# Pool mixer by band matrices on TensorE, and two chunks of the output projection as native four-byte products

## The chip, the cores and the metric

The kernel runs on one NeuronCore of a Trainium2 chip, batch 1. The metric is the device time of one execution in microseconds. Engines are named as in the profile: PE is TensorE, DVE VectorE, ACT ScalarE, POOL GpSimd, SP the engine whose queue issues every load.

## The reference

A sequence of 256 tokens of width 1024 goes through two transformer blocks. The first has stick-breaking and latent attention, a gated feed-forward part with a short convolution, and a per-token embedding gate. The second block, in which the change lies, computes

```
z   = (rmsnorm(x) * (1 + sc1) + sh1) @ w_in
y_conv = silu(layernorm(depthwise_conv31(val * sigmoid(gate))))   # 256 channels
y_att  = sparse attention: top 64 keys of each query by an index score   # 512 channels
y_pool = pool mixer of u_pool                                     # 256 channels
x  = x + g1 * (concat(y_conv, y_att, y_pool) @ w_out)
x  = x + g2 * mixture_of_experts(rmsnorm(x) ...)   # 32 experts, two of them for a token
out = rmsnorm(x)
```

The pool mixer has four groups of 64 channels with windows w = 2, 4, 8, 16. For each it computes the mean over the last min(t + 1, w) tokens minus the token itself, multiplies the 64 channels by a 64 x 64 matrix and scales them:

```
y_pool[t, group] = ((cs[t] - cs[t - w]) / min(t + 1, w) - u[t]) @ pool_w[group] * pool_scale
```

## The kernel before

Tokens come in two blocks of 128 (TB[b]), channels in chunks of 128. Weights arrive as 1 MB loads into three raw buffers (pool wr). For most products a weight is split into two halves that TensorE takes in one pass (hi, a cast by ScalarE, and lo, the rest, a subtraction by VectorE; function split, recorded on line 291), and so are the activations; mm3 (lines 273 to 275) then makes three products, hi x hi, hi x lo and lo x hi. Some products take four-byte operands as they are ("native"); the profile shows each of these as two records.

The order of TensorE's work is written out by hand: ORDER is a list of steps. Those that the text speaks of are `ix` (index scores), `cv` (conv inputs), `up` (the pool branch's input projection), `qk`, `va` (queries, keys and values), `d` (attention scores), `sm` (softmax), `po` (pool weights), `w0` to `w3` (load and split of the output weights, two chunks a load), `dT` (transposes of the attention weights), `do` (attention output), `c60` (chunk 6 of the output projection, block 0; chunks 0 and 1 are the conv's, 2 to 5 the attention's, 6 and 7 the pool's), `tp` (conv taps), `ct` and `co` (conv norm and output), and `ea`, `eh`, `el`, `e1` to `e4`, `es` (load a piece of the experts' weights into a buffer that has become free). Engines other than TensorE and the loads are put in order by a scheduler before the kernel runs, by priority (the order of the program) and by its own estimate of times; then each engine works strictly in that order. A buffer or a bank is given to the next user when the last reader of the one before is done. There are eight banks of PSUM: four take one block's scores, four the output projection's sums.

Index scores give 64 keys of each query: VectorE finds eight maxima and takes them out, eight times over (lines 1268 and 1269), for each block. Their mask goes into the maxima of the attention scores (line 803), whose exponentials, sums and normalised weights are ScalarE's, but for the negated maximum (line 806) and the reciprocal (line 810).

The Pool branch: `up_proj` makes the 256 channels with tokens along the free axis; GpSimd sums windows by shifted additions and a division (lines 1331 to 1341), `pool_out` multiplies by pool_w (line 1349) and splits the result into chunks 6 and 7 of mix2. The conv's 31 taps are multiply-adds of VectorE (line 1298); of the second half of its channels the last N_TAP taps are products of ScalarE (`pr`, six buffers) that GpSimd adds up (`cb`, line 1308).

The mixture of experts reads 192 pieces of 1 MB (`ew`), each into the next buffer of a ring. The ring is made of buffers of the mixer as they become free: its 23 pieces stand in ORDER and after it, in the order in which they are issued.

Of the kernel before, what the change touches and what calls it, by code (L numbers as in the profile page):

```python
# [38 lines left out]
N_TAP = 12  # L39
# [10 lines left out]
ORDER = 'qi0 kT0 qi1 kT1 ix0 ix1 cv0 li0 li1 cv1 ea ea lo0 lo1 ae lw ea ea ea va0 up eh el qk0 qk1 qk2 qk3 va1 d0 sm0 d1 po sm1 w3 e1 e2 c60 c61 w1 dT0 do0 c70 c71 c20 w2 dT1 c30 do1 tp e3 e4 e4 rl g1 c21 c31 c40 w0 ct e1 e1 c50 c51 c41 es es co'  # L50
# [17 lines left out]
def block_pair_kernel(ctx, tc, A, out, dbg=None):  # L68
# [126 lines left out]
    winv = cp.tile([P, 2], F32, name="winv")  # L195
    for i, wdt in enumerate((2, 4, 8, 16)):
        G.memset(winv[64 * (i % 2):64 * (i % 2) + 64, i // 2:i // 2 + 1], 1.0 / wdt)
    rcp = cp.tile([P, 2, PW], F32, name="rcp")
    G.iota(rcp[:, 0, :], pattern=[[1, PW]], base=1, channel_multiplier=0, allow_small_or_imprecise_dtypes=True)
    V.reciprocal(rcp[:, 0, :], rcp[:, 0, :])  # L200
    V.tensor_scalar(rcp[:, 1, :], rcp[:, 0, :], winv[:, 1:2], None, op0=ALU.max)
    V.tensor_scalar(rcp[:, 0, :], rcp[:, 0, :], winv[:, 0:1], None, op0=ALU.max)
# [1109 lines left out]
    TS = slice(PW, PW + SEQ)  # L1312
    pw = wk.tile([P, 2, 64], F32, name="pw")
    load(pw, A["pool_w"])
    pooled = []

    def up_proj():
        upb = bank("pup")
        raw = raw_pk("w_in2_c", 4, (2, KC, P), "r_up")
        for j in range(2):  # L1320
            ch_unit(raw[:, j], upb[:, j * SEQ:(j + 1) * SEQ], hZ, f"w_up2{j}")
        pu, s_a, s_b = [w2k2(nm).rearrange("p (c t) -> p c t", c=2) for nm in ("pu", "s_a", "s_b")]
        for t_ in (pu, s_a, s_b):
            G.memset(t_[:, :, 0:PW], 0.0)
        S.copy(pu[:, :, PW:], upb.rearrange("p (c t) -> p c t", c=2))

        def sh(t, c, rs, k):
            return t[rs, c, PW - k:PW + SEQ - k]

        full, top = slice(0, P), slice(64, P)  # L1330
        G.tensor_tensor(s_a[:, :, TS], pu[:, :, TS], pu[:, :, PW - 1:PW + SEQ - 1], op=ALU.add)
        G.tensor_tensor(s_b[:, 1, TS], sh(s_a, 1, full, 0), sh(s_a, 1, full, 2), op=ALU.add)
# [588 lines left out]
```

## Time and profile before

| | us |
|---|---|
| median of 3 runs | 942.63 (941.95 to 943.38) |
| the profiled execution | 942.79 |
| its span | 941.1 |
| PE busy | 785.0 |
| DVE busy | 466.7 |
| ACT busy | 321.8 |
| POOL busy | 110.1 |

The busy times are sums over the whole span. The mixer of the second block lies between about 380 and 490 us, the experts behind it. Times in the rows are microseconds from the start of the span.

### The profile page before, as it was taken

To read this page: it belongs to the slowest core of one execution; us is meant where nothing else is said; L and a number is where in the kernel's file an instruction comes from. 1 tells how busy PE (TensorE), PEld (TensorE's weight loads), DVE (VectorE), ACT (ScalarE), POOL (GpSimd) and SP (SyncE) were. 2 spreads that over 40 slices of the span, in tenths; PEclk is the share of its full clock that TensorE was granted. 3 is DMA by queue.
4 is the path that set the end of the run, shared out by engine and by line. 5 is a ranking of instruction groups with operands and counts; after the bars stand their busy time and mean duration, and the time that the engine had idled before them with its cause. 6 is when DMAs were issued, how large, how long until landed. Compare 5 with 4: busy or idle time off the path is not lost. (4 is left out here: it accounts for less than half of the span.)

```text
span 941.1 us, 17238 instructions
## 1 busy us (share of the span) xinstructions
PE 785.0 (83%) x7172; PEld 570.9 (61%) x7172; DVE 466.7 (50%) x1011; ACT 321.8 (34%) x636; POOL 110.1 (12%) x176
## 2 busy tenths in 40 slices
PE   6999989999999998996988988677766767766864
PEld 6898859999999775894675645243333433433422
DVE  5777476678888788589963323112121121211113
ACT  5649645555555575465741101000010000100100
POOL 1321320222112112207010000000000000000000
PEclk9999999999999998997999999879799897988887
DMA  8862388588676755745389999999999999999994
GB/s 309 283 206 85 122 333 318 194 338 313 254 276 231 268 203 194 301 168 179 129 332 422 422 420 425 419 425 421 423 422 422 425 422 422 423 421 426 420 423 166
DMA packets 45894, 301.22 MB, mean 320 GB/s; under 512 B 5360, under 2 KB 6388, under 8 KB 11124
## 3 DMA queue, kind: packets, MB, share of 16 engines
q1 hardware_dynamic: 45812, 300.08, 79.9%
q8 instruction: 58, 0.95, 0.4%
q14 instruction: 24, 0.20, 0.1%
HBM read 299.01 MB, written 1.05 MB: 319 GB/s over the span
## 5 line engine op out<-in xcount | busy, mean ns | idle before, releaser
L1710 PE MATMUL eu<-ew,XT 128*32 128x256 f32 x2048 | 141.8, 409 | 51.6 <-DMA ew<-in_exp_dram 51.5
L1710 PEld LDWEIGHTS eu<-ew,XT 128*32 128x32 f32 x2048 | 60.9, 115 | 123.9 <-DMA ew<-in_exp_dram 57.0
L80 ACT ACTIVATE hm<-eu 128x128 f32<-128x128 f32 x32 | 8.9, 278 | 334.2 <-PE eu L1710 334.2
L1737 PE MATMUL ey<-ew,hmT 128*32 128x256 f32 (+2 forms) x1088 | 80.7, 432 | 37.1 <-DMA ew<-in_exp_dram 25.2
L1723 DVE TENSOR_TENSOR hm<-hm,eu 128x128 f32<-128x128 f32 x32 | 9.2, 288 | 145.4 <-ACT hm L80 145.4
L1737 PEld LDWEIGHTS ey<-ew,hmT 128*32 128x32 f32 x1088 | 33.1, 121 | 71.6 <-DMA ew<-in_exp_dram 34.8
L1748 DVE TENSOR_TENSOR eys<-ey,g2y 128x256 f32<-128x256 f32 x31 | 13.2, 425 | 107.5 <-PE ey L1737 107.5
L1008 POOL TENSOR_TENSOR ac<-cv_g,cv_v 128x256 f32<-128x256 f32 x22 | 36.0, 1637 | 154.3 <-ACT w_g_w L80 108.3
L222 POOL TENSOR_SCALAR ep_fin<-msf 128x2 f32<-128x2 f32 x1 | 0.2, 238 | 446.2 <-DVE msf L1827 446.2
L275 PE MATMUL u<-hF_h,w_g_w 128*128 128x256 f32 x168 | 47.6, 283 | 0.0
L273 PE MATMUL u<-hF_h,w_g_w 128*128 128x256 f32 x168 | 47.5, 283 | 0.0
L274 PE MATMUL u<-hF_l,w_g_w 128*128 128x256 f32 x168 | 47.5, 283 | 0.0
L274 PE MATMUL u<-hF_l,w_v_w 128*128 128x256 f32 x160 | 45.3, 283 | 0.0
L275 PE MATMUL u<-hF_h,w_v_w 128*128 128x256 f32 x160 | 45.3, 283 | 0.0
L273 PE MATMUL u<-hF_h,w_v_w 128*128 128x256 f32 x160 | 45.2, 283 | 0.0
L1639 PE MATMUL moe<-eys,gT 32*128 32x256 f32 (+1 forms) x528 | 43.4, 444 | 1.4 <-DVE eys L1761 1.4
L1720 DVE COPY gT<-pgs 128x256 f32<-128x256 f32 x32 | 13.6, 425 | 52.4 <-PE pgs L1706 52.3
L80 ACT ACTIVATE XT<-px,c_SH,c_G 128x128 f32<-128x128 f32 x32 | 14.7, 458 | 63.9 <-DVE XT L1681 63.9
L1673 PEld LDWEIGHTS px<-hr,x 128*128 128x128 f32 x256 | 33.0, 212 | 4.3 <-issue 3.3
L1673 PE MATMUL px<-hr,x 128*128 128x128 f32 x256 | 34.7, 299 | 0.7 <-DVE hr L1665 0.7
L274 PE MATMUL dn<-w_dn_w,ach 128*128 128x512 f32 x88 | 34.6, 393 | 0.0
L1639 PEld LDWEIGHTS moe<-eys,gT 32*128 32x128 f32 x528 | 28.8, 216 | 9.5 <-issue 7.0
(566 smaller groups left out, 1978.1 us busy)
## 6 DMA issues: line engine op xcount, KB each, us to landing
ew<-in_exp_dram SPq DMA_DIRECT2D x189, 1024.0 KB, 19.7
r_mod<-in_mod_w_dram SPq DMA_DIRECT2D x24, 1024.0 KB, 8.7
r_gv<-in_w_up_dram SPq DMA_DIRECT2D x22, 1024.0 KB, 6.3
r_d<-in_w_down_dram SPq DMA_DIRECT2D x11, 1024.0 KB, 5.0
r_wo<-in_w_o_dram SPq DMA_DIRECT2D x4, 1024.0 KB, 4.8
r_pg<-in_w_ple_gate_dram SPq DMA_DIRECT2D x4, 1024.0 KB, 6.1
r_out<-in_w_out_dram SPq DMA_DIRECT2D x4, 1024.0 KB, 4.8
r_v<-in_w_in_t_dram SPq DMA_DIRECT2D x2, 1024.0 KB, 7.2
```

The source lines that it names most:

```text
L80: i = getattr(nc.scalar, name)(*a, **kw)
L273: T.matmul(o, l[0], r[0], start=start, stop=False, skip_group_check=True)
L274: T.matmul(o, l[0], r[1], start=False, stop=False, skip_group_check=True)
L275: T.matmul(o, l[1], r[0], start=False, stop=stop, skip_group_check=True)
L1008: G.tensor_tensor(a_, gt, vl, op=ALU.mult)
L1639: T.matmul(moe[c][:, b * 256:b * 256 + 256][:, js], gT[rs, TB[b]], yt[rs, js], start=(start and b == 0), stop=stop, skip_group_check=True)
L1673: T.matmul(pt[:, j * P:(j + 1) * P], x[b][:, k * P:(k + 1) * P], hr[:, b], start=(b == 0), stop=(b == 1))
L1710: T.matmul(u[32 * g_:32 * g_ + 32, 0:2 * P], XT[:, k, 32 * i:32 * i + 32], etiles[6 * e + k // 2][k % 2][:, :, P * g_:P * g_ + P], start=( ...
L1720: V.tensor_copy(gT, pg[:, :SEQ])
L1723: V.tensor_mul(hm, hm, u[:, P:2 * P])
L1737: T.matmul(y[32 * c:32 * c + 32, 0:64 * (js.stop - js.start)], hmT[:, 32 * k:32 * k + 32], w2e[k].rearrange("p j (c i) -> p c j i", c=4)[: ...
L1748: V.tensor_mul(yt, y[:, 0:256], g2y)
```

## The change

The window means become products with band matrices. A matrix `band` of each window has 1/w on its w diagonals, less one on the main one; `edge` holds the first 16 columns of the first block, where fewer than w tokens exist. They are built once by GpSimd and VectorE. `up_proj` now gives tokens along the partitions (puT), `pool_band` multiplies them by the bands, with the result again in channels by tokens, and `pool_out` leaves one four-byte tile (mixP) in place of two halves. Chunks 6 and 7 of the output projection multiply mixP by the rows of w_out as they were loaded; those rows are not split, and their raw buffer is read until the last such product. N_TAP goes from 12 to 20. In ORDER a step `pb` (pool_band) stands behind `qk1`, and `po` before `d1` in place of after it. Casts of the other output weights are ordered behind the last score copies (`first=[list(qk_ins)]`, an order on ScalarE alone).

```diff
-N_TAP = 12
+N_TAP = 20
...
-ORDER = '... up eh el qk0 qk1 qk2 qk3 va1 d0 sm0 d1 po sm1 w3 e1 e2 c60 c61 w1 dT0 do0 c70 c71 c20 w2 dT1 ...'
+ORDER = '... up eh el qk0 qk1 pb qk2 qk3 va1 d0 sm0 po d1 sm1 w3 e1 e2 c60 c61 w1 dT0 do0 c70 c71 c20 w2 dT1 ...'
...
-    winv = cp.tile([P, 2], F32, name="winv")
...
-    V.tensor_scalar(rcp[:, 0, :], rcp[:, 0, :], winv[:, 0:1], None, op0=ALU.max)
...
+    WIN = (2, 4, 8, 16)
+    band, edge = wk.tile([P, 4, P + 16], F32, name="band"), wk.tile([P, 4, 16], F32, name="edge")
+    rt = wk.tile([P, 16], F32, name="rt")
+    G.iota(rt, pattern=[[1, 16]], base=1, channel_multiplier=0, allow_small_or_imprecise_dtypes=True)
+    V.reciprocal(rt, rt)
+    for i, wdt in enumerate(WIN):
+        G.memset(band[:, i], 1.0 / wdt)
+        V.tensor_scalar(edge[:, i], rt, 1.0 / wdt, None, op0=ALU.max)
+    for t_, n in ((band, P + 16), (edge, 16)):
+        G.affine_select(t_, t_, pattern=[[0, 4], [1, n]], compare_op=ALU.is_ge, fill=0.0, base=0, channel_multiplier=-1)
+        for i, wdt in enumerate(WIN):
+            if wdt < n:
+                G.affine_select(t_[:, i], t_[:, i], pattern=[[-1, n]], compare_op=ALU.is_ge, fill=0.0, base=wdt - 1,
+                                channel_multiplier=1)
+        m = min(n, P)
+        V.tensor_sub(t_[:, :, :m], t_[:, :, :m], ident[:, None, :m].to_broadcast([P, 4, m]))
+    puT, pooled, mixP = [w2k2(nm)[:, :2 * SEQ].rearrange("p (c t) -> p c t", c=2) for nm in ("puT", "pooled", "mixP")]
...
     def up_proj():
-        upb = bank("pup")
-        raw = raw_pk("w_in2_c", 4, (2, KC, P), "r_up")
-        for j in range(2):
-            ch_unit(raw[:, j], upb[:, j * SEQ:(j + 1) * SEQ], hZ, f"w_up2{j}")
...
+        raw = raw_pk("w_in2_u", 0, (KC, 256), "r_up")
+        o = [bank(f"pup{b}") for b in range(NB)]
+        tok_unit(raw, 256, [t[:, :256] for t in o], hZ, "w_up2")
+        for b in range(NB):
+            S.copy(puT[:, b], o[b][:, :256])
+
+    def pool_band():
+        pb = bank("pband")
         for c in range(2):
...
+            o = pb[:, c * SEQ:(c + 1) * SEQ]
+            for b, cs_, t_, j in ((0, slice(0, 16), edge, 0), (0, slice(16, P + 16), band, 16), (1, slice(P, SEQ), band, 0)):
+                for par in range(2):
+                    rs = slice(64 * par, 64 * par + 64)
+                    T.matmul(o[rs, cs_], puT[:, b, 128 * c + 64 * par:][:, :64],
+                             t_[:, 2 * c + par, j:j + cs_.stop - cs_.start], start=(c == b == 0 and t_ is edge),
+                             stop=True, skip_group_check=True)
+        S.copy(pooled, pb.rearrange("p (c t) -> p c t", c=2))
...
-                hi, lo = [t[rs, 6 + c, :] for t in mix2]
-                act(hi, src, AF.Copy, scale=g_)
-                V.scalar_tensor_tensor(lo, src, g_, hi.bitcast(F32), op0=ALU.mult, op1=ALU.subtract)
+                act(mixP[rs, c, :], src, AF.Copy, scale=g_)
...
+        qk_ins[:] = [S.copy(q2[0][:, c, :], o[:, :SEQ]), S.copy(k2T[:, c, :], o[:, SEQ:])]
...
     def out_weights(u):
         raw = raw_rows("w_out_2", u, f"r_out{u}")
+        if u == 3:
+
+            wpo.update({6 + j: raw[:, j, :] for j in range(2)})
+            return
         for j in range(2):
-            wpo[2 * u + j] = split(raw[:, j, :], f"w_out{2 * u + j}", (D,), eng=G if 2 * u + j in OUT_G else V)
+            wpo[2 * u + j] = split(raw[:, j, :], f"w_out{2 * u + j}", (D,), eng=G if 2 * u + j in OUT_G else V,
+                                   first=[list(qk_ins)])
...
-        row_unit(wpo[c], [t[:, c, TB[b]] for t in mix2], acc[b], b not in begun, False)
+        if c < 6:
+            row_unit(wpo[c], [t[:, c, TB[b]] for t in mix2], acc[b], b not in begun, False)
+        else:
+            for n in range(2):
+                T.matmul(acc[b][n], mixP[:, c - 6, TB[b]], wpo[c][:, H2[n]], start=b not in begun, stop=False,
+                         skip_group_check=True)
```

## Rows read from the trace of the kernel before

**Rows 1.** The page's slices: GB/s moved in each fortieth of the span.
```profile
GB/s 309 283 206 85 122 333 318 194 338 313 254 276 231 268 203 194 301 168 179 129 332 422 422 420 425 419 425 421 423 422 422 425 422 422 423 421 426 420 423 166
```

**Rows 2.** Windows: stretch, length, busy of PE, PEld, DVE, ACT, POOL; clock, DMA share, GB/s.
```profile
425.00:435.00 10.00, 6.82 (x38) 4.95 (x38) 10.00 (x26) 6.41 (x15) 9.53 (x10) 0.90 0.61 210
...
445.00:450.00 5.00, 4.14 (x9) 2.84 (x10) 4.89 (x20) 4.04 (x12) 0.00 (x0) 0.50 0.00 2
450.00:465.00 15.00, 14.04 (x101) 10.41 (x99) 13.79 (x32) 12.44 (x31) 0.73 (x1) 0.99 0.14 45
465.00:480.00 15.00, 15.00 (x83) 11.88 (x81) 9.36 (x22) 7.27 (x12) 1.59 (x4) 1.00 1.00 391
480.00:485.00 5.00, 5.00 (x29) 4.15 (x27) 4.63 (x8) 2.55 (x7) 1.03 (x2) 1.00 0.40 165
```

**Rows 3.** SP's queue: two issues (timeline), a wait (total, times, longest), r_out's landing time.
```profile
461.76 0.33 SPq L142 DMA_DIRECT2D ew<-in_exp_dram  x1
...
484.34 0.33 SPq L142 DMA_DIRECT2D ew<-in_exp_dram  x1
...
SPq L142 <- PE ppt_d L827: 22.7, 1, 22.7
...
r_out<-in_w_out_dram SPq DMA_DIRECT2D x4, 1024.0 KB, 4.8
```

**Rows 4.** Timeline of PE: start, us, engine, line, operation, count, idle before and its releaser.
```profile
442.71 1.54 PE L1349 MATMUL ppl<-s_a,pw 64*64 64x256 f32 x6 [4.14 <-POOL s_a L1341]
...
448.11 0.63 PE L274 MATMUL mo<-w_out_w,mix_h 128*128 128x512 f32 x1
448.54 0.63 PE L275 MATMUL mo<-w_out_w,mix_l 128*128 128x512 f32 x1
...
450.92 0.27 PE L827 MATMUL ppt_d<-ident,es 128*128 128x128 f32 x1
```

**Rows 5.** The page's slices: POOL's busy tenths.
```profile
POOL 1321320222112112207010000000000000000000
```

**Rows 6.** Timeline of ACT.
```profile
430.67 1.04 ACT L80 CAST w_out_w<-r_out 128x1024 fp32r<-128x1024 f32 x1 [2.40 <-DMA r_out<-in_w_out_dram]
...
441.28 0.40 ACT L80 ACTIVATE es<-es,nm_d 128x128 f32<-128x128 f32 x1 [6.49 <-DVE nm_d L806]
...
445.85 2.45 ACT L80 ACTIVATE es<-es,rc_d 128x128 f32<-128x128 f32 x8 [0.18 <-DVE rc_d L810]
```

**Rows 7.** Timeline of DVE.
```profile
417.87 1.22 DVE L291 TENSOR_TENSOR w_out_w<-r_out,w_out_w 128x1024 fp32r<-128x1024 f32 x1
...
424.32 1.41 DVE L291 TENSOR_TENSOR w_out_w<-r_out,w_out_w 128x1024 fp32r<-128x1024 f32 x1
...
438.41 0.27 DVE L803 CUSTOM_DVE_ANT_0 es<-sc_d,ixb 128x128 f32<-128x128 f32 x1
...
441.06 4.65 DVE L1298 SCALAR_TENSOR_TENSOR ca<-upad,cols,ca 128x256 f32<-128x256 f32 x9
...
445.63 0.19 DVE L810 RECIPROCAL rc_d<-sum_d 128x8 f32<-128x8 f32 x1
```

**Rows 8.** Timeline of PE: native products, and three-pass products at full clock.
```profile
427.34 1.03 PE L1370 MATMUL pq<-lv,r_wu 128*128 128x256 f32 x4
428.20 0.59 PE L1371 MATMUL pq<-lv,r_wu 128*128 128x256 f32 x2
428.63 1.02 PE L1377 MATMUL pv<-r_wu,lv 128*128 128x512 f32 x2
...
454.41 0.40 PE L275 MATMUL mo<-w_out_w,mix_l 128*128 128x512 f32 x1
454.64 0.39 PE L273 MATMUL mo<-w_out_w,mix_h 128*128 128x512 f32 x1
```

**Rows 9.** Groups of POOL: count, busy us, mean ns, idle before them by releaser.
```profile
L1308 POOL TENSOR_TENSOR cb<-cb,pr 128x256 f32<-128x256 f32 x11 | 9.5, 866 | 3.1 <-ACT pr L80 2.3
...
L1008 POOL TENSOR_TENSOR ac<-cv_g,cv_v 128x256 f32<-128x256 f32 x22 | 36.0, 1637 | 154.3 <-ACT w_g_w L80 108.3 <-DVE cv_v L994 39.3 <-ACT w_dn_w L80 6.7
```

More of the change, by code (lines that the diff above doesn't have):

```diff
@@ L49 @@
 LAST = 'y01 y12 x2 m02 y24 m24'
-ORDER = 'qi0 kT0 qi1 kT1 ix0 ix1 cv0 li0 li1 cv1 ea ea lo0 lo1 ae lw ea ea ea va0 up eh el qk0 qk1 qk2 qk3 va1 d0 sm0 d1 po sm1 w3 e1 e2 c60 c61 w1 dT0 do0 c70 c71 c20 w2 dT1 c30 do1 tp e3 e4 e4 rl g1 c21 c31 c40 w0 ct e1 e1 c50 c51 c41 es es co'
+ORDER = 'qi0 kT0 qi1 kT1 ix0 ix1 cv0 li0 li1 cv1 ea ea lo0 lo1 ae lw ea ea ea va0 up eh el qk0 qk1 pb qk2 qk3 va1 d0 sm0 po d1 sm1 w3 e1 e2 c60 c61 w1 dT0 do0 c70 c71 c20 w2 dT1 c30 do1 tp e3 e4 e4 rl g1 c21 c31 c40 w0 ct e1 e1 c50 c51 c41 es es co'
 W_AT = (2,)
@@ L194, in block_pair_kernel @@
     PW = 16
-    winv = cp.tile([P, 2], F32, name="winv")
[L196 to L201, printed above, removed]
-    V.tensor_scalar(rcp[:, 0, :], rcp[:, 0, :], winv[:, 0:1], None, op0=ALU.max)
     slots = cp.tile([P, CAP], F32, name="slots")
@@ L1309, in conv_taps @@
         G.tensor_tensor(ca[:, 1, :], ca[:, 1, :], cb, op=ALU.add)
-    TS = slice(PW, PW + SEQ)
     pw = wk.tile([P, 2, 64], F32, name="pw")
     load(pw, A["pool_w"])
-    pooled = []
-    def up_proj():
-        upb = bank("pup")
-        raw = raw_pk("w_in2_c", 4, (2, KC, P), "r_up")
-        for j in range(2):
-            ch_unit(raw[:, j], upb[:, j * SEQ:(j + 1) * SEQ], hZ, f"w_up2{j}")
[L1322 to L1332, printed above, removed]
-        G.tensor_tensor(s_b[top, 0, TS], sh(s_a, 0, top, 0), sh(s_a, 0, top, 2), op=ALU.add)
-        G.tensor_copy(s_a[top, 0, TS], s_b[top, 0, TS])
-        G.tensor_tensor(s_a[:, 1, TS], sh(s_b, 1, full, 0), sh(s_b, 1, full, 4), op=ALU.add)
-        G.tensor_tensor(s_b[top, 1, TS], sh(s_a, 1, top, 0), sh(s_a, 1, top, 8), op=ALU.add)
-        G.tensor_copy(s_a[top, 1, TS], s_b[top, 1, TS])
-        G.tensor_tensor(s_a[:, :, PW:2 * PW], s_a[:, :, PW:2 * PW], rcp, op=ALU.mult)
-        for c in range(2):
-            G.tensor_scalar(s_a[:, c, 2 * PW:], s_a[:, c, 2 * PW:], winv[:, c:c + 1], None, op0=ALU.mult)
-        G.tensor_tensor(s_a[:, :, TS], s_a[:, :, TS], pu[:, :, TS], op=ALU.subtract)
-        pooled.append(s_a)
@@ L1348, in pool_out @@
                 rs = slice(64 * par, 64 * par + 64)
-                T.matmul(pb[par][rs, c * SEQ:(c + 1) * SEQ], pw[rs, c, :], pooled[0][rs, c, TS], start=(c == 0),
+                T.matmul(pb[par][rs, c * SEQ:(c + 1) * SEQ], pw[rs, c, :], pooled[rs, c, :], start=(c == 0),
                          stop=True, skip_group_check=True)
@@ L1365, in lat_load @@
         lw.extend(wu[:, 2 * i:2 * i + 2] for i in range(2))
+    qk_ins = []
     def qk2(c):
@@ L1455, in block_pair_kernel @@
     M2 = {}
-    steps = {"lw": lat_load, "up": up_proj, "po": pool_out, "tp": conv_taps, "ct": conv_T,
+    steps = {"lw": lat_load, "up": up_proj, "pb": pool_band, "po": pool_out, "tp": conv_taps, "ct": conv_T,
              "co": conv_out, "rl": router_load, "ea": lambda: grow(ewa, 1),
@@ L1885, in lay_out @@
     w = I["w_in_2"][0]
-    o["w_in2_c"] = ch(w, *((a, a + P) for a in (0, 256, 896, 1152, 1480)))
+    o["w_in2_c"] = ch(w, *((a, a + P) for a in (0, 256, 896, 1152)))
+    o["w_in2_u"] = tok(w, [(1480, 256)])
     o["w_in2_q"] = tok(w, [(512, 256)])
```

2 lines of the change are left out of this document (removed).

## The prediction

> **What bounds the kernel now.** I began with the page's slices [rows 1]: from the 22nd slice on the DMA engines move about 422 GB/s to the end, so from there the time is that of the stream of expert weights, and no engine can shorten it. What the change can move is the moment at which that stream becomes continuous. The windows [rows 2] and the queue [rows 3] place it. The DMA engines stand still at 445 to 450 us, run again, and sag at 480 to 485: 165 GB/s x 5 us are 0.83 MB, 2.0 us of work at 422 GB/s, so some 3 us of that window are empty. Every 1.05 MB piece waits for a buffer that the mixer lets go: one waits 22.7 us, up to 461.76, for the transposes of the attention weights, and the last large group is issued at 484.34, when the last products of the output projection have read their operands. From there on the rate has no gap. So the mixer's end moves the whole time one for one, as long as the pieces before it move too; the empty stretches in front of them leave room for that.
>
> Then I followed the mixer back from 484.34, engine by engine. TensorE is busy in 14.04 of 15 us from 450 to 465 and in all 15 from 465 to 480 [rows 2]: from the first transposes of the sparse attention (step dT0, 450.92 [rows 4]) to 484.34 it is its own bound, 33.4 us of work in a fixed order. What sets 450.92? Two things meet. First, dT0 stands in the order behind the twelve products of chunk 6 (c60, c61). These had to wait for the Pool branch: TensorE stood 4.14 us until GpSimd's last subtraction released it at 442.71, and then ran the chunk at half clock, 0.43 us from start to start [rows 4], the granted clock at 0.50 [rows 2]. Second, dT0 needs the normalised weights, which ScalarE has at 445.85 + 2.45 = 448.30 [rows 6]. They hang on a chain of VectorE: eight rounds of top-8 selection, the maxima of the scores from 438.41, the exponentials on ScalarE from 441.28, the reciprocal at 445.63 [rows 6, 7]. VectorE has no pause in it (10.00 of 10 us at 425 to 435 [rows 2]), so each instruction that stands between two of the chain's lengthens it.
>
> **The change part by part.**
>
> *The Pool branch.* Its eleven operations leave GpSimd. In their place stand twelve products of 64 output channels over 16, 144 and 128 columns. A four-byte product leaves two records; four records of 256 columns start at 427.34 and the next pair at 428.20, so a record takes 0.86 / 4 = 0.215 us, and a product of 512 columns 2 x 2 x 0.215 = 0.86 us at full clock [rows 8]. The band products have 4 x 288 = 1152 columns, 1.95 us one after another, half of it if the two halves of the array overlap. TensorE is busy in only 6.82 of 10 us at 425 to 435 [rows 2], because it waits for copies of ScalarE and then for the Pool branch; that wait covers the 1 to 2 us, and without it they would be on the path in full. The input projection keeps its 48 products of 256 columns. The product with the pool weights moves ahead of block 1's scores, and its results are there before chunk 6 can start at all, since the four banks of the output projection come free only when VectorE reads block 0's scores.
>
> *Chunk 6 runs earlier.* Its first bank is free about 1 us after the maxima begin, so at 437.3 if they begin at 436.3 (below). Four native products of 512 columns are 4 x 1.72 = 6.9 us at half clock, 3.4 at full: TensorE is free by 444.2 at the latest, and dT0 waits for its weights alone. That is worth 450.92 - 448.30 = **2.6 us**.
>
> *Two weight splits leave VectorE's chain.* Chunks 6 and 7 need none; theirs are the 1.22 us at 417.87 and the 1.41 us at 424.32 [rows 7]. The first stands before any tap is ready, so nothing follows it; into the second gap a tap will move, 4.65 / 9 = 0.52 us [rows 7]. Gain 1.22 + 0.89 = **2.1 us**, and dT0 moves on to 448.30 - 2.1 = 446.2. Bounds: 0, if other splits fill both places; 2.6, if nothing does.
>
> *Eight more taps go to ScalarE and GpSimd, and four low halves of chunks 6 and 7 vanish*, some 12 x 0.5 = 6 us of VectorE. The nine taps from 441.06 hold the reciprocal until 445.63, past the eight exponentials, which at 0.40 us each from 441.28 end at 444.5: 1.1 us that fewer taps could give back. I take 0; bounds 0 and 1.1. On GpSimd nineteen additions from 422 on at 0.87 us [rows 9] end at 439, long before the conv is needed. On ScalarE 8 x 0.4 to 0.5 us come on, two casts go, and it idles 6.49 us before 441.28 [rows 6].
>
> *Making the bands.* An iota, four fills and nine selections on GpSimd, five small operations and two subtractions on VectorE. At the price of an addition of 256 columns, 0.87 us [rows 9], nine selections of up to 576 columns are 8 to 18 us on GpSimd, which is idle in the slice before its branch (23.5 us, digit 0 of the 18th slice [rows 5]); VectorE's part is some 1.5 us, while TensorE works through projections. I take 0; bound 1.5, if VectorE does them inside the selection.
>
> *Chunk 7 after dT0.* It is on the path: one row block of three-pass products is 6 x 0.23 = 1.38 us [rows 8], the native one 2 x 0.86 = 1.72. Two blocks cost **+0.7 us** at full clock. At half clock they would take 6.9 us in place of 2.8: +4.1, the bound.
>
> *A raw buffer is kept.* There are three. The rows of chunks 6 and 7 hold theirs until TensorE has read them in c71, where now the next load follows their split; an expert piece takes another for good. Chunks 2 and 3 therefore wait for the third, that of the latent weights, read until 428.63 + 1.02 = 429.65 [rows 8] and, behind the band products, about 431.5; with 4.8 us to land [rows 3] they come at 436.3, where now ScalarE's wait for them ends at 430.67 [rows 6]. They are needed only after dT0, and the load behind c71 only for the last chunks. I take 0; the bound is the first rival. The new ordering rule puts the casts behind the score copies, which takes away the 2.40 us for which ScalarE stood on that load [rows 6] with copies queued behind it, and TensorE waiting for those.
>
> Sum: dT0 -2.6 - 2.1 = -4.7, chunk 7 +0.7, the mixer's end **-4.0 us**. The profiled execution took 942.79 (span 941.1), 0.16 above the median 942.63: 942.6 - 4.0 = **938.6**.
>
> **The rivals.** (1) *The kept buffer swallows the gain.* If VectorE's order has the low halves of chunks 2 and 3 inside the selection, it waits there for a load that comes 436.3 - 430.7 = 5.6 us later than now. That costs from 0 to 5.6; at 4 us dT0 is at 450.2, and the end at 942.6 - 0.7 + 0.7 = 942.6. For it: the order is fixed by a scheduler beforehand, and ScalarE stood 2.40 us on this load already. Against it: the scheduler knows the buffer. Half clock in chunk 7 (+4.1) ends at the same time.
>
> (2) *VectorE's relief is used in full.* If block 0's maxima, whose selection is done long before, move in among the rounds, the path follows VectorE's whole relief, 2.6 + 6 = 8 us and some: 934.5. Against it: the scheduler put taps in those gaps until now, though the scores were there.
>
> (3) *The other side: ScalarE is held by GpSimd.* Its tap products have six buffers; each further one waits for an addition. An addition of the same size takes 1.64 us in the feed-forward part, against 0.87 here [rows 9]. At 1.64 the eight new ones hold ScalarE 8 x 0.77 = 6.2 us, with score copies or exponentials queued behind them: the weights come at 446.2 + 6.2 = 452.4, 1.5 us later than dT0 now, and with chunk 7's 0.7 the time is 944.8. From 4 us of delay (1.37 us an addition) the gain is gone, from 5.9 it is slower by 0.2%. For it: that row. Against it: the 0.87 was taken beside the same taps. The Trainium skill, SBUF — State Buffer, section Who interferes with whom, says that a VectorE instruction with two SBUF inputs contends with a GpSimd instruction that reads SBUF; taps and additions are such a pair, and by it more additions beside fewer taps need not stay at 0.87. No row here separates that.
>
> **How the numbers follow.** The sum's case, 936.5 to 940.5: 0.55. Swallowed, 941 to 944: 0.22. Used in full, about 934.5: 0.10. Held, from 944 on: 0.13. 0.2% is 1.9 us, about what a measurement of this kernel can tell. Faster than that, below 940.7: 0.55 + 0.10 = 0.65; same 0.22; slower 0.13. With about a tenth left out at each end the range is 934.3 to 944.2.
>
> **What would show it.** Right: block 0's maxima near 436.3, c60 without a wait for GpSimd, dT0 near 446.2, the pieces of 484.34 near 480.3 and a full rate from there; chunk 7 in eight records of some 0.43 us. Wrong: VectorE or ScalarE waiting for the load of chunks 2 and 3 inside the selection; ScalarE waiting on conv additions ahead of copies or exponentials; a clock of 0.50 beyond dT0; or a mixer that ends earlier while the stream doesn't, because a load behind c71 holds the queue.

## The result, and the profile after

The changed kernel takes 948.24 us (median of 4 runs, 946.65 to 949.1), the kernel before beside it on the same chip 942.29 us: ratio 1.0062, 95% interval 1.0047 to 1.0077. It is 5.9 us slower, where 4.0 us faster had been predicted. The profiled execution, the longest of the four, took 949.1 us, span 947.2, so the two spans differ by 6.1 us.

**The stream still sets the end.** In the page's slices the rate rises to about 422 GB/s a slice later than before [rows 1] and then stays:

```profile
GB/s 310 296 212 61 133 329 298 193 343 311 255 279 225 268 209 184 319 145 72 223 339 393 422 419 424 419 424 420 422 424 421 424 420 422 424 420 424 421 420 157
```

Adding up the rate of all ten-us windows, 165.44 MB are left at 540 us, against 163.39 MB before: 2.05 MB, 4.9 us at 422 GB/s, of the 6.1. The windows of the changed kernel (columns as in [rows 2]) show where they were lost:

```profile
440.00:445.00 5.00, 1.61 (x7) 1.44 (x9) 4.93 (x24) 0.19 (x1) 0.89 (x2) 0.50 0.01 2
...
455.00:460.00 5.00, 5.00 (x22) 3.12 (x23) 4.26 (x10) 5.00 (x17) 0.00 (x0) 0.67 0.63 210
...
485.00:490.00 5.00, 5.00 (x37) 4.49 (x36) 3.89 (x6) 3.75 (x10) 1.12 (x2) 1.00 0.48 146
505.00:510.00 5.00, 3.90 (x63) 2.03 (x67) 2.90 (x12) 0.73 (x2) 0.00 (x0) 1.00 0.94 324
510.00:515.00 5.00, 5.00 (x78) 2.92 (x74) 1.71 (x6) 0.00 (x0) 0.00 (x0) 1.00 0.95 382
```

TensorE is busy in only 1.61 of 5 us at 440 to 445, the gap ahead of the stream lies in 485 to 490 instead of 480 to 485 [rows 2], and the stream thins once more at 505 to 515, where it had 424 and 421 GB/s before. SP's queue says the same (timeline): the group of pieces of 484.34 [rows 3] is issued at 487.60, and the rows of the output weight come late:

```profile
432.69 0.33 SPq L142 DMA_DIRECT2D r_out<-in_w_out_dram  x1
...
454.36 0.33 SPq L142 DMA_DIRECT2D r_out<-in_w_out_dram  x1
...
487.60 0.33 SPq L142 DMA_DIRECT2D ew<-in_exp_dram  x1
...
505.02 0.33 SPq L142 DMA_DIRECT2D ew<-in_exp_dram  x1
```

**What TensorE did.** Its timeline, to be read against [rows 4] and [rows 8]; most line numbers are eight lower than before for the same code:

```profile
427.83 0.64 PE L1338 MATMUL pband<-band,puT 128*64 128x128 f32 x8
...
436.05 1.04 PE L767 MATMUL sc_d<-qk 64*128 64x128 f32 x8 [2.75 <-ACT qk L80]
437.02 1.20 PE L1348 MATMUL ppl<-pooled,pw 64*64 64x256 f32 x8
438.15 1.22 PE L767 MATMUL sc_d<-qk 64*128 64x256 f32 x4
443.39 3.35 PE L767 MATMUL sc_d<-qk 64*128 64x256 f32 x12 [4.01 <-DVE mx_d L795]
446.66 4.40 PE L1415 MATMUL mo<-r_out,mixP 128*128 128x512 f32 x8
450.90 1.24 PE L819 MATMUL ppt_d<-ident,es 128*128 128x128 f32 x8
454.98 1.98 PE L833 MATMUL o_d<-es,lv 128*64 128x128 f32 x16 [2.85 <-DVE es L824]
456.89 4.40 PE L1415 MATMUL mo<-r_out,mixP 128*128 128x512 f32 x8
```

The band products are as cheap as predicted, and the Pool branch waits for nobody. But three waits have taken the place of the 4.14 us for GpSimd [rows 4]: 2.75 us for copies of queries and keys, 4.01 us for the banks that VectorE's maxima release, 2.85 us for VectorE's copy of the transposes. Chunk 6 starts at 446.66 (445.73 before) and dT0 at 450.90 (450.92 before). Counted from the first product of queries and keys, which itself came 1.5 us later (425.00 against 423.45), dT0 is 1.6 us sooner than before, and the mixer's loss stands behind it: from dT0 to the products with the values pass 4.08 us, and in the kernel before 1.38:

```profile
452.30 1.62 PE L841 MATMUL o_d<-es,lv 128*64 128x128 f32 x16 [0.34 <-DVE es L832]
```

**What VectorE did** (timeline, against [rows 7]):

```profile
435.14 0.81 DVE L1263 TENSOR_SCALAR ixb<-ixa 128x256 f32<-128x256 f32 x1
435.87 7.04 DVE L1290 SCALAR_TENSOR_TENSOR ca<-upad,cols,ca 128x256 f32<-128x256 f32 x10
442.83 0.28 DVE L795 CUSTOM_DVE_ANT_0 es<-sc_d,ixb 128x128 f32<-128x128 f32 x1
...
449.08 0.20 DVE L802 RECIPROCAL rc_d<-sum_d 128x8 f32<-128x8 f32 x1
...
451.90 1.22 DVE L283 TENSOR_TENSOR w_out_w<-r_out,w_out_w 128x1024 fp32r<-128x1024 f32 x1
...
453.11 1.22 DVE L283 TENSOR_TENSOR w_out_w<-r_out,w_out_w 128x1024 fp32r<-128x1024 f32 x1
454.24 0.68 DVE L824 COPY es<-ppt_d 128x512 f32<-128x512 f32 x1
```

The selection's chain did get shorter: its mask (block 1's, the last), at 438.61 us before, is made at 435.14. Not only the splits of chunks 6 and 7 have left it: those of chunks 2 and 3, at 433.31 and 435.62 in the kernel before, now stand at 451.90 and 453.11, right ahead of the copy of block 0's transposes. Behind the mask come ten taps in a row, 0.70 us each on average, and block 0's maxima start at 442.83 instead of 438.41.

**What ScalarE did** (timeline, against [rows 6]): products for GpSimd stand among the copies of queries and keys and wait for GpSimd's additions, 1.9 us in all; the last copies start at 435.38, block 0's exponentials at 445.11 instead of 441.28.

```profile
434.96 0.51 ACT L80 ACTIVATE pr<-upad,cols 128x256 f32<-128x256 f32 x1 [0.36 <-POOL cb L1300]
435.38 1.17 ACT L80 COPY qk<-pq 128x256 f32<-128x256 f32 x4
...
445.11 0.40 ACT L80 ACTIVATE es<-es,nm_d 128x128 f32<-128x128 f32 x1 [4.92 <-DVE nm_d L798]
```

Of the 6.1 us some 1.5 are older than the mixer: in the profiled execution of the changed kernel everything from the first feed-forward on is that much later, which is told at the end. From the first product of queries and keys to the group of pieces at 487.60 pass 62.6 us, 1.7 more than before; the next issue (505.02) comes another 0.7 later, and most of the rest is lost in the thin windows up to 515.

### The profile page after: what moved, and what is told of

Its sections match the earlier page's. It is cut to its first block, busy times and chain, and to the rows that moved or that the text cites. A ratio compares the mean times of both kernels' runs of the same rounds, so it can differ in the third digit from the quotient of the medians.

```text
span 947.2 us, 17274 instructions
## 1 busy us (share of the span) xinstructions
PE 791.6 (84%) x7188; PEld 572.7 (60%) x7188; DVE 461.2 (49%) x1001; ACT 323.7 (34%) x644; POOL 108.1 (11%) x179
## 5 line engine op out<-in xcount | busy, mean ns | idle before, releaser
L1718 PE MATMUL eu<-ew,XT 128*32 128x256 f32 x2048 | 139.2, 402 | 58.6 <-DMA ew<-in_exp_dram 58.6
L1745 PE MATMUL ey<-ew,hmT 128*32 128x256 f32 (+2 forms) x1088 | 88.0, 463 | 29.5 <-DMA ew<-in_exp_dram 17.7
L1647 PE MATMUL moe<-eys,gT 32*128 32x256 f32 (+1 forms) x528 | 40.0, 414 | 1.3 <-DVE eys L1769 1.3
L1681 PEld LDWEIGHTS px<-hr,x 128*128 128x128 f32 x256 | 36.7, 231 | 5.5 <-issue 4.5
L1681 PE MATMUL px<-hr,x 128*128 128x128 f32 x256 | 38.4, 319 | 0.7 <-DVE hr L1673 0.7
L80 ACT ACTIVATE XT<-px,c_SH,c_G 128x128 f32<-128x128 f32 x32 | 14.6, 457 | 70.1 <-DVE XT L1689 70.1
L266 PE MATMUL dn<-w_dn_w,ach 128*128 128x512 f32 x88 | 34.6, 393 | 0.0
L265 PE MATMUL dn<-w_dn_w,ach 128*128 128x512 f32 x88 | 34.5, 393 | 0.0
```

The lines of the kernel that those rows point to most:

```text
L80: i = getattr(nc.scalar, name)(*a, **kw)
L265: T.matmul(o, l[0], r[0], start=start, stop=False, skip_group_check=True)
L266: T.matmul(o, l[0], r[1], start=False, stop=False, skip_group_check=True)
L1647: T.matmul(moe[c][:, b * 256:b * 256 + 256][:, js], gT[rs, TB[b]], yt[rs, js], start=(start and b == 0), stop=stop, skip_group_check=True)
L1681: T.matmul(pt[:, j * P:(j + 1) * P], x[b][:, k * P:(k + 1) * P], hr[:, b], start=(b == 0), stop=(b == 1))
L1718: T.matmul(u[32 * g_:32 * g_ + 32, 0:2 * P], XT[:, k, 32 * i:32 * i + 32], etiles[6 * e + k // 2][k % 2][:, :, P * g_:P * g_ + P], start=( ...
```

## The experiments

Five theories were to be told apart. Theory 1: the place that the change freed on VectorE was filled with taps, ahead of block 0's maxima. Theory 2: the native chunks at half clock. Theory 3: the kept raw buffer. Theory 4: the eight further shared taps (4a through ScalarE's order, 4b through GpSimd's additions beside VectorE's taps). Theory 5: the pool products ahead of block 1's scores. Each kernel was timed beside the kernel before on the same chip, whose median was 943.8 to 944.2 us there (942.29 beside the changed kernel). The ratio is estimated from all executions of both kernels and is not the quotient of the two medians. "Mixer" is the stretch from the first product of queries and keys to the group of expert pieces that [rows 3] has at 484.34, in the one execution that was profiled; it takes out what differs ahead of the mixer. It is 60.9 us in the kernel before, 62.6 in the changed one.

| run | median, us | ratio to before, 95% interval | mixer, us |
|---|---|---|---|
| changed kernel | 948.24 | 1.0062 (1.0047 to 1.0077) | 62.6 |
| e1_hold13 | 944.0 | 0.9997 (0.9984 to 1.0011) | 57.8 |
| e2_ntap12 | 942.36 | 0.9988 (0.9977 to 0.9999) | 57.9 |
| e3_po_late | 954.58 | 1.0110 (1.0093 to 1.0127) | 71.4 |
| e4_split67 | 947.23 | 1.0044 (1.0028 to 1.0059) | 63.3 |
| e5_hold13_ntap12 | 940.2 | 0.9951 (0.9930 to 0.9971) | 54.8 |
| e6_before_native67 | 952.95 | 1.0087 (1.0060 to 1.0113) | 67.9 |
| e7_before_ntap20 | 948.06 | 1.0044 (1.0023 to 1.0065) | 64.1 |
| e8_bands_split_cured | 946.27 | 1.0005 (0.9987 to 1.0024) | 59.3 |
| e9_native67_copyfirst | 947.55 | 1.0037 (1.0025 to 1.0049) | 62.5 |
| e10_ntap20_prlate | 946.28 | 1.0023 (1.0013 to 1.0033) | 62.0 |
| e11_w1late_copyfirst | 939.22 | 0.9951 (0.9933 to 0.9970) | 53.4 |
| e12_hold8 | 942.64 | 0.9977 (0.9964 to 0.9989) | 57.1 |
| e13_ntap1 | 941.51 | 0.9974 (0.9960 to 0.9987) | 56.4 |
| e14_before_ntap1 | 950.23 | 1.0055 (1.0036 to 1.0075) | 65.1 |
| e15_cured_ntap8 | 940.48 | 0.9968 (0.9953 to 0.9983) | 54.9 |

**e1_hold13**: the changed kernel, the taps held.

```diff
+                    done += 1
+                    if done > 13:
+                        after(t_, mx_ins['d0'])
```

> The changed kernel with one bound put on VectorE's order: every tap of the convolution after the 13th may only stand behind the last of block 0's maxima, so the ten taps of 435.87 to 442.83 us move behind them. Theory 1 (the order of VectorE: the freed place was taken by taps): block 0's maxima start when its scores are there, at about 436 to 437 instead of 442.83, block 1's scores find free banks 4 to 5 us sooner, the transposes of block 0 start at about 446 instead of 450.90, and the time falls by 3 to 5 us, to 943 to 945. Theory 2 (the two native chunks, 4.40 us each, set the mixer's length) and theory 3 (the kept raw buffer makes rows of the output weight late): no more than 1 us comes off, 947 to 948.5, because the chunks and the loads stand where they stood.

The loss is gone: 0.9997. On TensorE (timeline) block 1's scores no longer wait for banks, and chunk 6 starts 16.7 us after the first query product (422.18) instead of 21.7 (446.66 after 425.00); the first wait, for the copies, is still there.

```profile
433.35 1.04 PE L767 MATMUL sc_d<-qk 64*128 64x128 f32 x8 [2.83 <-ACT qk L80]
...
435.50 3.46 PE L767 MATMUL sc_d<-qk 64*128 64x256 f32 x16
438.89 3.70 PE L1421 MATMUL mo<-r_out,mixP 128*128 128x512 f32 x8
```

Theory 1 named the wait; the order of VectorE is enough to undo the loss.

**e2_ntap12**: the changed kernel with `N_TAP = 12`.

> The changed kernel with 12 taps shared to ScalarE and GpSimd as before, not 20. Theory 1 (taps ahead of block 0's maxima on VectorE): 11 of them still stand there, so the maxima stay at 442 to 443 us and the time at 947 to 949. Theory 4 (ScalarE held by GpSimd's additions: the copies of the queries and keys stand behind products that wait, the last copy at 435.38 instead of 433.62): the copies come 1.5 to 2 us sooner, taps that run beside fewer GpSimd additions cost 0.52 instead of 0.70 us, and the time falls by 1.5 to 3 us, to 945 to 946.7.

More than theory 4 expected: 0.9988. Eleven taps still stand ahead of the maxima, but they take 4.43 us in a row, 0.40 each (the ten of the changed kernel 7.04), TensorE has no wait for the copies left (the wait for banks stays, 4.69 us), and the maxima start at 438.06, 14.6 us after the first query product instead of 17.8. So theory 1 alone is too simple: the taps in front do harm because they are long, and they are long because GpSimd adds beside them.

**e3_po_late**: the pool products behind block 1's scores, in the changed kernel.

```diff
-d0 sm0 po d1 sm1
+d0 sm0 d1 po sm1
```

> The changed kernel with the pool branch's products behind block 1's scores again, as before. Theory 5 (they stand between the two blocks' scores, and chunk 6 and block 1's scores are late for that, the wait for banks of 4.01 us): 1 to 2 us come off, 946 to 947. Theory 1 (taps on VectorE ahead of block 0's maxima): the wait for banks ends on those maxima wherever the pool branch's products stand, so the time is 947 to 949, or later by up to 2 us if the scaling on ScalarE falls behind the exponentials and chunk 6 waits for it.

Theory 5 is refuted, and the time is 6 us above the changed kernel's, more than any theory allowed. Chunk 6 does wait for the scaling on ScalarE, as theory 1 allowed (3.43 us), but the waits of TensorE at 425 to 475 us show one that nobody expected:

```profile
PE o_d L833 <- ACT es L80: 6.5, 2, 6.0
```

ScalarE's copy of the second bank of block 0's transposes had been put behind block 1's exponentials and their normalisation. The scheduler fixes this order beforehand; the hand-written order of TensorE does not bind it. This became theory 6: ScalarE's order.

**e4_split67**: the changed kernel with chunks 6 and 7 of split weight and rows (`u == 3` splits as the others, `out_chunk` uses `row_unit` alone).

> The changed kernel, its band matrices kept, with chunks 6 and 7 of the output projection as three products of split weight and rows again, as before; the raw buffer is free again after the split. Theory 2 (the native chunks at half clock, 4.40 us each against about 2.8 us for twelve products at the full clock): chunk 7 gets shorter and the time falls by 1 to 2 us. Theory 3 (the kept buffer): the next rows of the output weight are issued at 426 to 430 instead of 432.69 us, the copy at 454.24 no longer stands behind two late splits, and 1 to 2.5 us come off. Both: 944 to 946. Theory 1 (taps ahead of the maxima): the maxima stay at 442 to 444 us since nine taps and a split stand ahead of them, and the time is 947.5 to 950.

1.0044 against 1.0062, intervals that overlap: no difference that was measured, as theory 1 had it. Nine taps and a split stand ahead of the maxima, which start at 443.29. Theory 3 is not tested by it: the rule that holds the casts behind the score copies stayed in, so the splits of chunks 6 and 7 came at 442.15 and 446.08, the raw buffer was not free sooner, and the next rows were issued at 432.46, as in the changed kernel (432.69).

**e5_hold13_ntap12**: both cures, e1's bound and e2's 12 taps.

> The changed kernel with both cures: taps after the 13th held behind block 0's maxima, and 12 taps shared to ScalarE and GpSimd instead of 20. Theory 1 with theory 4 as two causes (the place of the taps; and GpSimd's additions, which hold the copies of queries and keys on ScalarE and stretch VectorE's taps from 0.40 to 0.70 us): the gains add, block 0's maxima stand 2 to 3 us sooner than in the run that only held the taps, the transposes of block 0 about 16 to 18 us after the first query product instead of 20.3, and the time is 1.5 to 3.5 us under either cure alone, 939 to 941.5. Rival: both cures take away one and the same wait, and the next one (the split of late rows of the output weight ahead of the copy of the transposes, chunk 7 at half clock) takes over: 942 to 944.

940.2 us, ratio 0.9951: each cure gains on top of the other, though the two together give less (1.1%) than the sum of what each gives alone (0.65% and 0.74%). This version beats both kernels, by 0.5% and 1.1%. Chunk 6 starts where the prediction had drawn it (437.3) and dT0 4 us sooner (446.2 in the prediction), but from dT0 to the products with the values pass 4.84 us, against 1.38 in the kernel before:

```profile
435.42 1.98 PE L767 MATMUL sc_d<-qk 64*128 64x256 f32 x12 [0.34 <-DVE mx_d L797]
437.33 2.84 PE L1421 MATMUL mo<-r_out,mixP 128*128 128x512 f32 x6
440.88 1.12 PE L1421 MATMUL mo<-r_out,mixP 128*128 128x512 f32 x2 [0.71 <-ACT mixP L80]
442.26 2.38 PE L821 MATMUL ppt_d<-ident,es 128*128 128x128 f32 x8 [0.25 <-ACT es L80]
447.10 1.33 PE L835 MATMUL o_d<-es,lv 128*64 128x128 f32 x16 [2.47 <-DVE es L826]
```

**e6_before_native67**: the kernel before with native chunks 6 and 7 alone.

> The kernel before with one part of the change alone: chunks 6 and 7 of the output projection as native four-byte products from unsplit rows, the pool branch still on GpSimd. As the prediction had it, the two splits that leave VectorE bring block 0's maxima 2.1 us forward, but chunk 6 still waits for GpSimd's pool branch at 442.7 us, so the time stays within 1 us of before, 942 to 944. Theory 3 (the kept raw buffer makes the next rows of the output weight 3 to 7 us late, and their splits stand ahead of the copy of the transposes): 944 to 946.5. Theory 1 (freed places on VectorE are taken by taps; the order here has eight of them ahead of the maxima): the maxima move by less than 1 us either way.

8.7 us slower, and none of the theories expected it. TensorE, then ScalarE (timelines):

```profile
459.78 1.97 PE L841 MATMUL o_d<-es,lv 128*64 128x128 f32 x14 [5.88 <-ACT es L80]
```

```profile
455.81 3.30 ACT L80 ACTIVATE es<-es,rc_d 128x256 f32<-128x256 f32 x8
459.14 0.59 ACT L80 COPY es<-ppt_d 128x512 f32<-128x512 f32 x1
```

Most of it is the wait of e3_po_late: the copy stands behind block 1's normalisation. In the kernel before it stood at 452.19, ahead of block 1's exponentials.

**e7_before_ntap20**: the kernel before with `N_TAP = 20` alone.

> The kernel before with one part of the change alone: 20 taps instead of 12 shared to ScalarE and GpSimd. GpSimd works on the pool branch until 442 us and on additions until 460 us already, so the eight further additions end at about 467 us, ahead of the transposes of the convolution at 470.65. If they only fill idle time: 942 to 944. Theory 4 (the products on ScalarE stand ahead of the copies of queries and keys and wait for GpSimd; GpSimd's additions stretch the taps): block 0's scores and maxima 1.5 to 4 us later and the time 945 to 948.

1.0044: the time of theory 4, but not by the maxima, which start at 438.13 (438.41 before). What comes late is behind them. ScalarE, then VectorE (timelines):

```profile
439.89 0.51 ACT L80 ACTIVATE pr<-upad,cols 128x256 f32<-128x256 f32 x1 [4.78 <-POOL cb L1308]
...
441.87 0.51 ACT L80 ACTIVATE pr<-upad,cols 128x256 f32<-128x256 f32 x1 [1.47 <-POOL cb L1308]
...
444.13 0.51 ACT L80 ACTIVATE pr<-upad,cols 128x256 f32<-128x256 f32 x1 [1.76 <-POOL cb L1308]
444.55 0.39 ACT L80 ACTIVATE es<-es,nm_d 128x128 f32<-128x128 f32 x1
```

```profile
440.78 7.93 DVE L1298 SCALAR_TENSOR_TENSOR ca<-upad,cols,ca 128x256 f32<-128x256 f32 x9
```

Products that wait for additions hold the exponentials until 444.55 (441.28 before), and the nine taps ahead of the reciprocal take 7.93 us instead of 4.65 [rows 7]. Single taps show why. First the kernel before: one tap and GpSimd's subtraction beside it; then e7: one tap and the addition beside it (timelines):

```profile
441.45 1.48 DVE L1298 SCALAR_TENSOR_TENSOR ca<-upad,cols,ca 128x256 f32<-128x256 f32 x1
441.30 1.35 POOL L1341 TENSOR_TENSOR s_a<-s_a,pu 128x512 f32<-128x512 f32 x1
```

```profile
445.17 0.94 DVE L1298 SCALAR_TENSOR_TENSOR ca<-upad,cols,ca 128x256 f32<-128x256 f32 x1
445.04 0.79 POOL L1308 TENSOR_TENSOR cb<-cb,pr 128x256 f32<-128x256 f32 x1
```

Both taps end 0.28 us after GpSimd's instruction (442.93 after 442.65, 446.11 after 445.83), and so, to within 0.01 us, do 186 of the 188 taps that begin beside an addition in the seventeen profiles. The other eight taps of the kernel before take 0.40 us from start to start; in e7 seven of the nine stand beside additions and take 0.75 to 0.98, mostly 0.87. ScalarE's products are not the cause: the last of them ends at 444.64, and the taps behind it stay as long.

**e8_bands_split_cured**: the band matrices as the only part, with both cures (edits of e1, e2 and e4 together).

> The changed kernel with the band matrices as its only part: chunks 6 and 7 of split weight and rows again, 12 taps shared, and the taps after the 13th held behind block 0's maxima. Against the run with both cures and native chunks it tells what the native chunks are worth by themselves. Theory 2 (native chunks cost 4.4 to 4.8 us each where the clock is low, against 2.8 to 5.2 us for twelve products): 0 to 1.5 us faster than that run. If the two splits and the four halves that come back to VectorE matter more: 1 to 3 us slower than that run.

1.0005, about 5 us behind e5: with the splits and low halves back on VectorE its last taps come late, and TensorE waits 2.69 us for them ahead of the convolution's transposes:

```profile
469.33 1.12 PE L1427 MATMUL pcl<-ident,ca 128*128 128x128 f32 x4 [2.69 <-DVE ca L1293]
```

Ahead of the products with the values it waits for VectorE too, 3.67 us (2.47 in e5). So in these surroundings the native chunks pay for themselves by what they take off VectorE, half clock or not.

**e9_native67_copyfirst**: e6 with ScalarE's order mended.

```diff
+                    c_ = S.copy(dst, pt)
+                    if name == 'd0':
+                        for e_ in exps['d1']:
+                            after(e_, c_)
```

> The kernel before with native chunks 6 and 7 alone, as in the run that took 952.95 us, and one bound on ScalarE's order: block 1's exponentials stand behind the copy of block 0's second bank of transposes. Theory 6 (the loss of 8.7 us is ScalarE's order: that copy stood behind block 1's exponentials, a cast and its normalisation, at 459.14 us, and the products with the values waited 5.88 us for it): that wait goes to under 1 us and the time falls by 4 to 7 us, to 946 to 949. Rival (the native chunks at half clock, 5.7 and 4.4 us, and the late rows of the output weight are the loss): less than 2 us come off, 951 to 953.

5.4 us come off (4.7 by the ratios), and the wait for ScalarE's copy is gone (1.6 us for VectorE's remain): theory 6 is shown. 0.37% remain. Chunk 6 still waits for GpSimd's Pool branch and then takes 5.93 us, so in the kernel before the native chunks are no gain.

**e10_ntap20_prlate**: e7 with ScalarE's last six products behind block 0's exponentials.

> The kernel before with 20 taps shared, as in the run that took 948.06 us, with ScalarE's last six products held behind block 0's exponentials. Theory 4a (ScalarE held by GpSimd: three of those products waited for GpSimd's additions and pushed the exponentials from 441.28 to 444.55): the exponentials start at 441 to 441.5 again, chunk 6 about 3 us sooner, and 2.5 to 4 us come off, 944 to 945.5. Theory 4b (VectorE's nine taps beside GpSimd's additions take 7.93 instead of 4.65 us, and the reciprocal of block 0's sums stands behind them at 448.63): the additions are still there, so less than 1.5 us come off, 946.5 to 948.5.

Between the two: 946.28, ratio 1.0023 against 1.0044. The exponentials come 17.9 us after the first query product (442.52 after 424.65), as before (441.28 after 423.45); the nine taps still take 5.71 us. So ScalarE's order (4a) is about half of e7's loss by the times, whose intervals overlap, and two thirds by the mixers (64.1, 62.0 and 60.9 us). The rest fits the additions (4b): the reciprocal still comes 23.3 us after the first query product, against 22.2 before.

**e11_w1late_copyfirst**: e5 with the splits of chunks 2 and 3 behind block 0's transposes and the edit of e9.

```diff
-c60 c61 w1 dT0 do0
+c60 c61 dT0 w1 do0
```

> The changed kernel with both cures (taps after the 13th held, 12 shared), and the splits of the next two rows of the output weight behind block 0's transposes instead of ahead, with block 1's exponentials held behind the second bank's copy so that ScalarE keeps its order. Theory 3 (the splits of rows that come late, at 443.41 and 445.22 us, keep VectorE's copy and the products with the values waiting 2.47 us): 1 to 2 us under the run with both cures, 938 to 939.5 beside a before of 944. Rival (chunk 2 then waits for those splits, or chunk 7 at half clock swallows it): 939.5 to 941.5.

The wait of 2.47 us falls to 0.85 and the mixer is 1.4 us shorter, but the ratio is the same, 0.9951. Theory 3's wait was real; what it is worth in time is less than these intervals (some 0.2%, 1.9 us, to either side) can show.

**e12_hold8**: e11 with `done > 8`.

> As the run with the splits late, with the taps after the 8th held instead of after the 13th, so that five fewer stand among the top-8 rounds, whose end (434.67 us) is what block 0's maxima wait for. If VectorE's chain from the top-8 rounds to the maxima sets the mixer: 1 to 2 us under that run, 936.5 to 938.5. Rival (the taps put off come back at the end, ahead of the transposes of the convolution, where the run with bands alone waited 2.69 us): no gain or up to 2 us more, 938.5 to 941.

0.9977, 3.4 us over e11 and more than the rival had; its mechanism is there: the taps put off come back ahead of the convolution's transposes, where TensorE now waits 3.79 us.

**e13_ntap1, e14_before_ntap1, e15_cured_ntap8**: `N_TAP = 1` in the changed kernel, in the kernel before, and `N_TAP = 8` in e11.

> The changed kernel with 1 shared tap instead of 20, so GpSimd makes no additions of products and VectorE has 59 taps instead of 40. Theory 4b (an addition on GpSimd stretches the taps beside it by as much as a tap costs): a tap takes 0.40 us throughout, VectorE's taps 24 us in all against 22.7 with 40 of them, and the time is within 1.5 us of the run with 12 shared, 941 to 944 beside a before of 944. Rival (the taps cost about 0.5 us each whatever GpSimd does): 59 of them take 30 us, the last ones stand ahead of the transposes of the convolution, and the time is 945 to 949.

> The kernel before with 1 shared tap instead of 12; GpSimd keeps its pool branch. Theory 4b: its 59 taps take VectorE 25 us or a little more, against 24.8 us for 48; the nine taps ahead of the reciprocal take 3.6 to 4 us instead of 4.65, the exponentials stay where they are, and the time is within 1.5 us of before, on either side. Rival: the eleven more taps cost 5 to 6 us, half of it on the path, 946 to 949.

> The changed kernel as in the run with both cures and the splits late (939.22 us), with 8 taps shared instead of 12. If four additions fewer take as much off the other taps as four taps put on, VectorE's load is unchanged and the time is within 1 us, 938.5 to 940.5. If VectorE's last taps now stand ahead of the transposes of the convolution: 941 to 943.

The price of a shared tap is settled by VectorE's group of taps from 405 to 475 us (count, busy us, mean ns), first the kernel before and e7 (12 and 20 shared), then the changed kernel, e2 and e13 (20, 12 and 1):

```profile
L1298 DVE SCALAR_TENSOR_TENSOR ca<-upad,cols,ca 128x256 f32<-128x256 f32 x48 | 24.8, 549 | 0.3
```

```profile
L1298 DVE SCALAR_TENSOR_TENSOR ca<-upad,cols,ca 128x256 f32<-128x256 f32 x40 | 24.6, 630 | 0.5
```

```profile
L1290 DVE SCALAR_TENSOR_TENSOR ca<-upad,cols,ca 128x256 f32<-128x256 f32 x40 | 22.7, 581 | 0.5
```

```profile
L1290 DVE SCALAR_TENSOR_TENSOR ca<-upad,cols,ca 128x256 f32<-128x256 f32 x48 | 22.8, 506 | 0.3
```

```profile
L1290 DVE SCALAR_TENSOR_TENSOR ca<-upad,cols,ca 128x256 f32<-128x256 f32 x59 | 24.9, 470 | 0.0
```

Moving eight taps to ScalarE and GpSimd frees 0.2 us of VectorE in the one kernel and 0.1 in the other; moving nineteen frees 2.2. Theory 4b is shown between 12 and 20 shared taps; between 1 and 12 the price is about half, since eleven more taps cost 2.1 us and not 11 x 0.40 = 4.4. That fits the single taps: among the top-8 rounds a tap meets only the rest of an addition, and its records there take 0.55 to 0.62 us in the changed kernel (0.47 alone, 0.94 beside a whole one). And e13 with 59 taps on VectorE is 0.26% faster than before. In the kernel before (e14) 59 taps take 25.8 us, 1.0 more than 48, as 4b has it, but the time is 1.0055 and not within 1.5 us: the last fourteen taps stand at the end, and the convolution's transposes wait 1.7 us for them and then 2.5 us for GpSimd's closing addition, which took 3.17 us beside two splits of VectorE (472.73 to 475.07) and 0.73 in the kernel before:

```profile
472.48 3.17 POOL L1309 TENSOR_TENSOR ca<-ca,cb 128x256 f32<-128x256 f32 x1 [37.02 <-DVE ca L1298]
```

For e15 the last taps are late too, a wait of 3.3 us; 0.9968 against 0.9951 is no measured difference.

## Why the prediction was wrong

**What bounds the kernel: right, but not one for one.** In all fifteen experiments and the changed kernel, the bytes left at 540 us give the difference of the span from before's to within 1.5 us. "One for one" from the mixer's end holds less well: from that group of pieces to the next issue pass 16.7 us in the profiled execution before (to 501.05), 17.4 in the changed kernel and 16.7 to 18.7 in the others, and with it the stream runs dry for a moment, as at 505 to 515 above. Across the runs the time against before is the mixer's difference plus 0 to 4 us, mostly 1 to 3 (e11: mixer 7.5 us shorter, time 4.6 us); in the changed kernel the mixer is 1.7 us longer and the time 5.9. Where these come from was not settled; the delay in before's profiled execution, with e3's the shortest of all, may be part of it.

**The Pool branch on TensorE: right.** The band products take 1.3 us under cover, making the bands is hidden, and the wait of 4.14 us for GpSimd is gone.

**Chunk 6 earlier, 2.6 us: right as a step, but it needs the maxima.** Its banks come free with them; with the maxima at 434.87 in e5 it starts at 437.33.

**Two splits leave the chain, 2.1 us: this is the first step that failed.** The chain shortened by more, 3.5 us by the clock of the traces and 5.0 from the first query product (15.2 to 10.1), since the splits of chunks 2 and 3 left it too. But the maxima, forecast at 436.3, came at 442.83, because "into the second gap a tap will move" was the wrong picture: ten taps stand between the mask and the maxima. With them held behind the maxima (e1) the loss is gone. Late scores on ScalarE are not what put them there: in e2 the scores are not late, and eleven taps stand there. Why the scheduler ordered them so was not shown.

**Eight more taps to ScalarE and GpSimd, taken at 0, bounds 0 and a gain of 1.1: the second.** It is a loss: 0.44% (4 us) when made alone in the kernel before, and taking it back from the changed kernel brings 1.0062 to 0.9988, 7 us; e1 takes back 6 us and both together 10.5, so the two steps share a part. A shared tap hardly relieves VectorE, since an addition on GpSimd costs the tap beside it about what a tap costs; and it holds ScalarE. The taps run at 0.40 us from start to start while GpSimd is idle (11 in 4.43 us in e2) and mostly at 0.87 beside additions; the mean of 0.70 in the changed kernel mixes the two. The prediction read the 0.87 us of an addition [rows 9] and took it that the additions would change nothing on VectorE. The trace before had the price: the 4.65 / 9 = 0.52 us that the prediction took for a tap [rows 7] is the mean of eight at 0.40 and one of 1.41 from start to start, the one beside GpSimd's subtraction, and the prediction's "No row here separates that" does not hold. The Trainium skill, SBUF — State Buffer, section Who interferes with whom, has a VectorE instruction with two SBUF inputs contend with a GpSimd instruction that reads SBUF; by that rule, which the prediction named only for its third rival, taps and additions contend, and these traces agree, with 0.40 us for a tap alone and mostly 0.87 beside an addition.

**Chunk 7, +0.7, bound +4.1: about right.** From its start to the next product it takes 3.84 us, against 2.9 for the twelve products before: +1.0, with the granted clock at 0.67 over 455 to 460.

**The kept buffer, taken at 0: the third.** The load was late as the prediction had it (issued at 432.69 against 425.76), and "needed only after dT0" was right for the rows but not for their splits: those stand ahead of the copy of the transposes, TensorE waits 2.85 us for that copy, and from dT0 to the products with the values pass 2.7 us more than before. Of the mixer, forecast 4.0 us shorter and measured 1.7 longer, that is about half of what was missed; the other half is dT0, 25.9 us after the first query product where the forecast had 22.8. What the late rows cost in time is open: e11 takes 1.4 us off the mixer and nothing measurable off the time, and e4 left the rows as late as they were.

**The rivals.** The third was the mechanism: ScalarE held by GpSimd and a slower pair of engines. But the prediction looked for it in longer additions (they took 0.80 us, not 1.64), and it was the taps that lengthened. The first came in another place: the late low halves stood not inside the selection but ahead of the copy of the transposes. Of the second, relief used in full, e5 and e11 show what was there once the order was held.

## What to carry to other kernels

Before you move work from one engine to another, look for two rows of the same instruction, one taken while the other engine was idle and one while it worked; their difference is the price of the move; here it was as large as the work, and both rows stood in the trace before, hidden in one mean. Where a scheduler fills the side engines' order, a shorter chain ends sooner only if what follows it is bound to follow: look for filler work that fits in the gap, hold it behind the critical instruction, and expect an edit elsewhere to shuffle an order that nobody wrote (e6 lost about 5 us to one copy that had slipped back). A part that loses in the old surroundings (native chunks, e6) can gain in the new ones (e5 against e8), so test parts in both.

## What was unexpected of the hardware

**The same products at two clocks in the same place.** The 1.5 us ahead of the mixer come from the stretch 140 to 145 us, in which both kernels run the same code (windows, before and then changed; columns as in [rows 2]):

```profile
140.00:145.00 5.00, 4.50 (x37) 4.38 (x37) 2.13 (x3) 1.05 (x1) 0.00 (x0) 1.00 0.92 344
```

```profile
140.00:145.00 5.00, 4.37 (x23) 4.37 (x24) 1.17 (x2) 0.55 (x1) 0.00 (x0) 0.57 0.93 336
```

TensorE had waited 3.3 and 3.4 us for VectorE up to 136.5 us; the granted clock is 1.00 in the one, the upper level of 2.4 GHz, and 0.57 in the other, mostly the lower of 1.2 GHz, and eight products take 1.12 or up to 2.08 us. In the fifteen experiments it lies between 0.60 and 1.00 there, with no edit in that code. A second such stretch is 90 to 100 us: 1.00 before, 0.81 and 0.85 in the changed kernel, which loses about 1.6 us there and had been about 1.5 us ahead. Over the seventeen profiles the first query product comes anywhere from 421.75 to 425.39 us, which is as much as the effects looked for; a difference of two single profiles is read only after that is taken out.

**Native chunks at three clocks.** Chunk 6 takes 3.70 us for its eight records in e1, 5.93 in e9 and 6.75 in e3, with the granted clock at 1.00, 0.61 and 0.53 from its start to the next product. In e1 TensorE had last waited 5.5 us before it began (2.83 us, up to 433.35); in e9 it had waited 8.72 us up to 439.50 and 2.76 right ahead of the chunk, in e3 4.57 up to 442.81 and 3.43 right ahead.
